# Both pooled halves ahead of the loop over heads, an encoder trunk on one core

## The chip, the cores and the metric

The kernel runs on one core of a Trainium2 chip. A core has five engines with an instruction queue each: TensorE (PE in the profile) multiplies matrices, VectorE (DVE), ScalarE (ACT) and GpSimd (POOL) work on tiles of 128 partitions, and SyncE (SP) issues most of the transfers. The metric is the time of one execution on the device, in microseconds (us).

## The reference, cut to what matters

A trunk of two layers over 512 tokens of 1024 channels, in float32. Each layer is a half-step feed-forward block, a mixing block and another half-step feed-forward block. The mixing block is what the change touches:

```python
proj = rmsnorm(x, mix_norm) @ w_in          # [v_pool 256 | q 768 | k 768 | v 768]
y_pool = multiscale_pool(v_pool, pool_w, pool_scale)
q, k = apply_partial_rope(q), apply_partial_rope(k)
y_attn = dilated_mixture_attention(q, k, v) # 12 heads of 64 channels
x = x + concat(y_pool, y_attn) @ w_out

def multiscale_pool(v):                      # windows 2, 4, 8, 16 for four groups of 64 channels
    mean_g = (running sum of v_g over the window) / (valid positions)
    return ((mean - v) @ pool_w_g) * pool_scale
```

## The kernel before, in words

The activations are held transposed: channels on the 128 partitions, the 512 tokens along the free axis. A tile of 128 channels is 128x512, and the 1024 mixed channels are eight tiles y[0] to y[7]: y[0] and y[1] are the two pooled halves, y[2] to y[7] the six pairs of heads. Each float32 product is made from operands that are split in a high and a low part, as three matmuls (`mm3`, lines 414 to 419: high x high, high x low, low x high). A split is two instructions: ScalarE copies the high part (line 435, or 387 for weights: `whi`), and VectorE subtracts it from the whole (line 438, or 390 for weights: `wlo`). Such second instructions are recorded as "rests" and are issued at the next `flush()`.

All engines run their queues in the order in which the program is written; no scheduler moves anything. In `mix(l)` that order is: `values` and `qk` of pair 0, then `pool(0)` and `qk(1, 0)`, each by `run`, which issues a generator's products in one piece; then the loop over 13 steps s of four quarters q. A step makes the scores and the exp of head s (`scores`; VectorE's pass with the row maxima is line 914, ScalarE's exp line 916), the transposes of the probabilities of head s-1 with their split (`weigh`: `ph` and `pl`), and the products with the values (`gather`). Between them `advance()` issues one piece (six matmuls) of the product that the table `fill` gives to the step: q or k of a later pair. In the last steps it also issues output products.

Three parts of the loop matter here:

- `pool(c)`: 24 matmuls (`pp_pool`), then VectorE's `v_pool` (line 983), then a chain on GpSimd: three memsets, running sums (line 992, two of them for c = 0 and four for c = 1), two scalings (lines 1004 and 1005) and a subtraction (line 1006) that gives `m_pool`. The generator stops at `yield "tail"`, and some yields later it splits the small weight (`pwh`, `pwl`) and `m_pool` (`dh_pool` on ScalarE, `dl_pool` on VectorE), and makes three matmuls (`po_pool`), from which ScalarE takes y[c].
- `qk(pr, s)`: 24 matmuls (`pp_q`, `pp_k`), VectorE's product with the cosines (`ra`, line 875) and shuffle (`rb`, 876), GpSimd's two instructions (lines 877 and 878), and the split `hl_q` or `hl_k`, which is then copied to the stacked operands by DMAs of SyncE.
- `prepare(c)` splits y[c] into `yh[c]` at the place that the table `plan` names, and `out(d, ks)` makes the products of output tile d with the mixed tiles ks, three matmuls for each, at the places of the table `work`. Both tables are keyed by (step, quarter).

The weights' order in the list of loads (`plain(*entry)`) is the order in which the products take them.

Of the kernel before, what the change touches and what calls it, by code (L numbers as in the profile page):

```python
# [78 lines left out]
def trunk(ctx: ExitStack, tc: tile.TileContext, a: dict):  # L79
    nc = tc.nc  # L80
# [168 lines left out]
    def plain(key, src, n):  # L249
        ld = Load(src, n)  # L250
        loads.append(ld)
        jobs.append(Job(key, n, [ld], lambda: ld.tile, done=free))
# [71 lines left out]
    def ffn_jobs(i, l):  # L324
        for n, u in enumerate(UNITS):
            if n == 0:
                for g in range(4):
                    plain(("c", i, l, g), a[f"gc{i}"][l, g], D)
                continue
            pj = product_jobs(i, l, u)  # L330
            dj = down_jobs(i, l, UNITS[n - 1]) if n else []
            for z, job in enumerate(pj):
                jobs.append(job)
                if n and z in DOWN_AT[n == len(UNITS) - 1]:
                    jobs.append(dj.pop(0))
            jobs.extend(dj)
        jobs.extend(down_jobs(i, l, UNITS[-1]))

    for l in range(DEPTH):
        ffn_jobs(1, l)  # L340
        vu = [[(("v", l, hf, g), a["wv"][l, hf, g], 768) for g in range(4)] for hf in range(2)]
        qk = [(("qk", l, p_, s), a["wqk"][l, p_, s], D) for p_ in range(NPAIR) for s in range(2)]
        pu = [(("p", l, c), a["wp"][l, c], D) for c in range(2)]
        wo = [(("o", l, d), a["wo"][l, d], D) for d in range(KD)]
        for entry in vu[0] + qk[:2] + vu[1] + pu[:1] + qk[2:] + pu[1:] + wo:
            plain(*entry)
        ffn_jobs(2, l)

# [84 lines left out]
    def split_later(dst, src, then=None, engine=nc.vector):  # L433
        hi, lo = dst
        nc.scalar.activation(hi, src, AF.Copy)

        def rest():
            engine.tensor_tensor(lo, src, hi.bitcast(F32), op=ALU.subtract)
            if then is not None:
                then()  # L440
        later.append(rest)
# [384 lines left out]
    def mix(l, norm, nxt):  # L826
# [5 lines left out]
        y = [None] * KD  # L832
        yh = [None] * KD
# [32 lines left out]
        def qk(pr, s, before=None, tag="A"):  # L866
            name = f"{'qk'[s]}_{nm}_{pr}"
            ps = bank(tag, f"pp_{name}")
            yield from project(take("qk", l, pr, s), ps)
            if before is not None:  # L870
                before()
                yield "tail"
            t = t2([P, S], F32, f"ra_{name}")
            sh = t2([P, S], F32, f"rb_{name}")
            nc.vector.tensor_tensor(t, ps, rc, op=ALU.mult)
            nc.vector.stream_shuffle(sh, ps, SWAP)
            nc.gpsimd.tensor_tensor(sh, sh, rsn, op=ALU.mult)
            nc.gpsimd.tensor_tensor(t, t, sh, op=ALU.add)
            hl = t4([P, 2, S], F32R, f"hl_{name}")
            yield "tail"  # L880
            if (pr, s) != (NPAIR - 1, 1):
                yield

            def stacks():
                for j in range(2):
                    hd = 2 * pr + j
                    src = hl[j * HD:(j + 1) * HD].bitcast(F32)
                    if s == 0:
                        st = t4([P, 2, S], F32R, f"qq_{nm}_{hd}")
                        nc.sync.dma_start(st[0:HD].bitcast(F32), src)  # L890
                        nc.sync.dma_start(st[HD:P].bitcast(F32), src)
                        qq[hd] = st
                    else:
                        st = t2([P, S], F32R, f"kk_{nm}_{hd}")
                        nc.sync.dma_start(st[0:HD].bitcast(F32), src[:, 0, :])
                        nc.sync.dma_start(st[HD:P].bitcast(F32), src[:, 1, :])
                        kk[hd] = st

            split_later(planes(hl), t, stacks)
# [66 lines left out]
        def prepare(c):  # L966
            if c in (1, 6, 7):
                yh[c] = (t2([P, S], F32R, f"yhh_{nm}_{c}"), t2([P, S], F32R, f"yhl_{nm}_{c}"))
            elif c in (2, 3):
                yh[c] = (t2([P, S], F32R, f"yhh_{nm}_{c}"), t2([P, S], F32R, f"yhl_{nm}_{c}"))  # L970
            else:
                yh[c] = planes(t4([P, 2, S], F32R, f"yh_{nm}_{c}"))
            split_later(yh[c], y[c], engine=nc.gpsimd if c in (0, 2, 3) else nc.vector)

        def pool(c, tag="A"):
            name = f"pool_{nm}_{c}"
            ps = bank(tag, f"pp_{name}")
            yield from project(take("p", l, c), ps)
            W = S + 16
            v = t4([P, W], F32, f"v_{name}")  # L980
            nc.gpsimd.memset(v[:, 0:8], 0.0)
            nc.gpsimd.memset(v[:, S + 8:W], 0.0)
            nc.vector.tensor_tensor(v[:, 8:S + 8], ps, norm.row, op=ALU.mult)
            ic = t2([P, S], F32, f"ic_{name}")
            nc.sync.dma_start(ic, a["icnt"][:, c])
            raw = t2([P, P], F32, f"pwr_{name}")
            nc.gpsimd.memset(raw, 0.0)
            for g in range(2):
                nc.sync.dma_start(raw[g * 64:(g + 1) * 64, g * 64:(g + 1) * 64], a["pool_w"][l, 2 * c + g])
            s = t4([P, W], F32, f"s_{name}")  # L990
            r = t4([P, W], F32, f"r_{name}")
            add = lambda o, i, sh, lo, n: nc.gpsimd.tensor_tensor(
                o[:, lo:lo + n], i[:, lo - sh[0]:lo - sh[0] + n], i[:, lo + sh[1]:lo + sh[1] + n], op=ALU.add)
            add(s, v, (1, 0), 1, W - 1)
            if c == 0:
                add(r, s, (1, 1), 8, S)
                first, second = s, r
            else:
                add(r, s, (1, 1), 2, W - 3)
                add(s, r, (2, 2), 4, W - 7)  # L1000
                add(r, s, (4, 4), 8, S)
                first, second = s, r
            m = t2([P, S], F32, f"m_{name}")
            nc.gpsimd.tensor_tensor(m[0:64], first[0:64, 8:S + 8], ic[0:64], op=ALU.mult)
            nc.gpsimd.tensor_tensor(m[64:P], second[64:P, 8:S + 8], ic[64:P], op=ALU.mult)
            nc.gpsimd.tensor_tensor(m, m, v[:, 8:S + 8], op=ALU.subtract)
            yield "tail"
            yield
            yield
            pw = (t2([P, P], F32R, f"pwh_{name}"), t2([P, P], F32R, f"pwl_{name}"))  # L1010
            split_later(pw, raw)
            yield
            yield
            d = (t2([P, S], F32R, f"dh_{name}"), t2([P, S], F32R, f"dl_{name}"))
            split_later(d, m)
            yield
            yield
            po_ = bank("D", f"po_{name}")
            mm3(po_, pw, 0, d, True, True)
            yc = t2([P, S], F32, f"y_{name}")  # L1020
            nc.scalar.activation(yc, po_, AF.Copy, scale=pscale(l, c))
            y[c] = yc

        wo, pso = {}, {}

        def out(d, ks):
            if d not in wo:
                wo[d] = take("o", l, d)
                pso[d] = bank("AABBCCAA"[d], f"po_{nm}_{d}")
            for k in ks:  # L1030
                mm3(pso[d], wo[d], k * P, yh[k], k == 0, k == 7)
# [16 lines left out]
        def run(gen):  # L1048
            live.append(gen)
            while True:  # L1050
                flush()
                if advance()[-1] is not None:
                    break
# [9 lines left out]
        run(qk(0, 1, tag="C"))  # L1063
        run(values(1))
        run(pool(0, tag="C"))
        run(qk(1, 0, tag="C"))
        fill = [qk(1, 1)]
        for p_ in range(2, NPAIR):
            fill += [qk(p_, 0), qk(p_, 1)]
        fill += [pool(1)]  # L1070

        plan = {(7, 3): (2,), (8, 2): (3,), (9, 1): (0,), (10, 0): (4,), (10, 2): (5,), (12, 0): (1,), (12, 2): (6,)}
        work = {(10, 0): ((0, (0, 2)),), (10, 1): ((1, (0, 2)),), (10, 2): ((0, (3, 4)),), (10, 3): ((1, (3, 4)),),
# [3 lines left out]
        state["behind"] = True  # L1077
        for s in range(NH + 1):
            if s < len(fill):
# [21 lines left out]
        flush()  # L1101
        gather(NH - 1, 2)
        out(0, (6,))
        out(1, (1, 6))
        gather(NH - 1, 3)
        flush()
        normalise(NPAIR - 1)
        flush()
        prepare(7)
        flush()  # L1110
        out(2, (1, 6))
        out(3, (6,))
        out(4, (0, 2, 3, 4, 5, 1, 6))
        for d in range(KD):
# [78 lines left out]
```

## Time and profile before

| | us |
|---|---|
| median of three runs | 1872.42 (1870.88 to 1872.94) |
| the profiled execution, its own time | 1871.56 |
| its span in the trace | 1869.2 |
| TensorE busy | 1851.1 (99%) |
| VectorE busy | 1403.0 (75%) |
| ScalarE busy | 934.2 (50%) |
| GpSimd busy | 117.6 (6%) |

The span is what the trace covers of the execution; the rest lies around it. The mixing block is a stretch of each of the two layers, and its loop over heads lies from 424.5 to 555.1 in layer 0. The busy time of TensorE counts overlapping matmuls once, so the rate at which matmuls start is read from their start times.

### The profile page before, as it was taken

The page shows a single profiled execution, that of the slowest core. Times are in us where ns is not written, and L with a number is a line of the kernel's source. Part 1 is how long each engine was busy: PE and PEld are TensorE (multiplying, and loading weights), DVE is VectorE, ACT ScalarE, POOL GpSimd, SP SyncE. Part 2 cuts the span into 40 slices and gives each one's busy share as a digit, 9 for nine tenths or more (in the row PEclk, how much of TensorE's full clock was granted, in tenths as well). Part 3 has the DMA queues.
Part 4 walks back from the last instruction along what each step waited for, and adds up shares of the span by engine and source line. Part 5 has one row for each costly group of instructions (what it writes and reads, how often), then busy time and mean ns, then how long its engine had stood idle before and what let it go on. Part 6 is the DMA issues. An engine that isn't in the chain of part 4 may idle for free.

```text
span 1869.2 us, 23006 instructions
## 1 busy us (share of the span) xinstructions
PE 1851.1 (99%) x8735; PEld 1537.4 (82%) x8735; DVE 1403.0 (75%) x1983; ACT 934.2 (50%) x1440; POOL 117.6 (6%) x104
## 2 busy tenths in 40 slices
PE   9999999999999999999999999999999999999998
PEld 7788888898878888888888888888887788888888
DVE  5888777748887887677698677775688697777675
ACT  6444444526665554444464344344467565444344
POOL 0000000014230000000000000000323200000000
PEclk8999999999999999999999999999999999999999
DMA  4332333144442232333403332230544223323321
GB/s 188 124 102 79 112 124 111 43 126 122 113 142 96 74 105 99 113 106 108 136 23 118 119 102 97 95 130 17 147 123 126 102 85 119 114 89 102 102 79 46
DMA packets 59375, 194.33 MB, mean 104 GB/s; under 512 B 8001, under 2 KB 8129, under 8 KB 59265
## 3 DMA queue, kind: packets, MB, share of 16 engines
q1 hardware_dynamic: 58720, 192.05, 32.0%
q8 instruction: 69, 1.13, 0.3%
q10 hardware_dynamic: 432, 0.56, 0.1%
q14 instruction: 42, 0.34, 0.1%
q0 software_dynamic: 112, 0.26, 0.0%
HBM read 171.87 MB, written 2.10 MB: 93 GB/s over the span
## 4 chain that ended last, share of the span: by engine, by line
PE 92%; DVE 5%; issue 1%; ACT 1%; DMA 0%; DVEq 0%; POOLq 0%; POOL 0%; ACTq 0%
PE pd_f L419 9%; PE pd_f L417 8%; PE pd_f L418 8%; PE px_f L710 7%; PE px_f L707 7%; PE px_f L709 7%; PE pz_f L710 6%; PE pz_f L707 6%; PE pz_f L709 6%; PE pv_m L844 4%; PE ps_m L911 2%; PE pt_m L924 2%; PE pt_f L656 2%; PE pc_f L752 2%; PE pc_f L754 2%; PE pc_f L753 2%
## 5 line engine op out<-in xcount | busy, mean ns | idle before, releaser
L390 DVE TENSOR_TENSOR wlo<-raw,whi 128x1024 fp32r<-128x1024 f32 (+2 forms) x414 | 489.9, 1189 | 50.8 <-ACT whi L387 46.5
L387 ACT ACTIVATE whi<-raw 128x1024 fp32r<-128x1024 f32 (+2 forms) x414 | 413.6, 1023 | 225.0 <-DVE wlo L390 67.7
L419 PE MATMUL pd_f<-ah_f,wlo 128*128 128x512 f32 (+1 forms) x736 | 281.2, 382 | 1.8 <-DVE wlo L390 1.7
L417 PE MATMUL pd_f<-ah_f,whi 128*128 128x512 f32 (+1 forms) x736 | 280.8, 382 | 0.0
L418 PE MATMUL pd_f<-al_f,whi 128*128 128x512 f32 (+1 forms) x736 | 279.6, 380 | 0.0
L802 DVE SCALAR_TENSOR_TENSOR x<-pd_f,x 128x512 f32<-128x512 f32 x184 | 127.0, 690 | 168.5 <-PE pd_f L419 165.0
L648 ACT ACTIVATE c_f<-c_f,rcol_n 128x256 f32<-128x256 f32 x120 | 61.2, 510 | 232.5 <-DVE c_f L689 87.5
L419 PEld LDWEIGHTS pd_f<-ah_f,wlo 128*128 128x128 f32 x736 | 138.3, 188 | 31.9 <-DVE wlo L390 6.1
L418 PEld LDWEIGHTS pd_f<-al_f,whi 128*128 128x128 f32 x736 | 138.5, 188 | 26.2
L417 PEld LDWEIGHTS pd_f<-ah_f,whi 128*128 128x128 f32 x736 | 138.5, 188 | 25.5
L710 PE MATMUL px_f<-wlo,sh_n 128*128 128x512 f32 x320 | 124.6, 389 | 1.7 <-DVE wlo L390 1.7
L710 PE MATMUL px_f<-wlo,ah_n 128*128 128x512 f32 x320 | 124.6, 389 | 0.0
L709 PE MATMUL px_f<-whi,sl_n 128*128 128x512 f32 x320 | 124.5, 389 | 0.0
L707 PE MATMUL px_f<-whi,sh_n 128*128 128x512 f32 x320 | 124.5, 389 | 0.0
L707 PE MATMUL px_f<-whi,ah_n 128*128 128x512 f32 x320 | 124.5, 389 | 0.0
L709 PE MATMUL px_f<-whi,al_n 128*128 128x512 f32 x320 | 124.5, 389 | 0.0
L707 PE MATMUL pz_f<-whi,sh_n 128*128 128x512 f32 x320 | 124.5, 389 | 0.0
L709 PE MATMUL pz_f<-whi,sl_n 128*128 128x512 f32 x320 | 124.5, 389 | 0.0
L710 PE MATMUL pz_f<-wlo,sh_n 128*128 128x512 f32 x320 | 124.5, 389 | 0.0
L916 ACT ACTIVATE e_m<-e_m,nmx_m 128x512 f32<-128x512 f32 x96 | 69.4, 723 | 81.3 <-DVE nmx_m L914 81.0
L914 DVE CUSTOM_DVE_ANT_0 e_m<-ps_m,gbias 128x512 f32<-128x512 f32 x96 | 65.9, 686 | 30.7 <-PE ps_m L911 29.9
L554 POOL TENSOR_TENSOR rcol_n<-rcol_n,npow 128x4 f32<-128x4 f32 x6 | 7.4, 1228 | 1197.0 <-DVE rcol_n L553 1197.0
(222 smaller groups left out, 3683.1 us busy)
## 6 DMA issues: line engine op xcount, KB each, us to landing
raw<-in_gu SPq DMA_DIRECT2D x160, 512.0 KB, 3.3
raw<-in_dn SPq DMA_DIRECT2D x80, 512.0 KB, 3.3
raw<-in_wqk SPq DMA_DIRECT2D x24, 512.0 KB, 5.4
qq_m<-hl_q_m SPq DMA_DIRECT2D x48, 256.0 KB, 4.3
raw<-in_wo SPq DMA_DIRECT2D x16, 512.0 KB, 5.0
raw<-in_gc SPq DMA_DIRECT2D x15, 512.0 KB, 4.2
raw<-in_wv SPq DMA_DIRECT2D x16, 384.0 KB, 3.1
kk_m<-hl_k_m SPq DMA_DIRECT2D x48, 128.0 KB, 2.3
```

The lines of the kernel that those rows point to most:

```text
L387: nc.scalar.activation(hi[:, o:e], raw[:, o:e], AF.Copy)
L390: nc.vector.tensor_tensor(lo[:, o:e], raw[:, o:e], hi[:, o:e].bitcast(F32), op=ALU.subtract)
L417: nc.tensor.matmul(ps, hi[:, o:o + P], act[0], start=start, stop=False)
L418: nc.tensor.matmul(ps, hi[:, o:o + P], act[1], start=False, stop=False)
L419: nc.tensor.matmul(ps, lo[:, o:o + P], act[0], start=False, stop=stop)
L707: nc.tensor.matmul(ps, bh, hi[:, o], start=(k == 0 and p in (1, 2, 5)), stop=False, skip_group_check=True)
L709: nc.tensor.matmul(ps, bl, hi[:, o], start=False, stop=False, skip_group_check=True)
L710: nc.tensor.matmul(ps, bh, lo[:, o], start=False, stop=(k == 3), skip_group_check=True)
L802: nc.vector.scalar_tensor_tensor(x[d], ps, 0.5, x[d], op0=ALU.mult, op1=ALU.add)
L844: nc.tensor.matmul(ps[t][:, :384], h[k][p_][:, t * P:(t + 1) * P], q_[:, o:o + 384], start=(k == 0 and n == 0), stop=(k == KD - 1 and n == 2))
L914: nc.vector.tensor_tensor_reduce(e, ps, gbias[:, o:o + S], -0.125, 3.0e38, ALU.add, ALU.min, nmx[hd][:, it:it + 1])
L916: nc.scalar.activation(e, e, AF.Exp, bias=nmx[hd][:, it:it + 1], scale=-1.0, accum_out=den[hd][:, it:it + 1])
```

## The change

`pool(1)` is run right after `pool(0)`, ahead of the loop, and leaves the table `fill`; its weight moves up in the list of loads. The tail of `pool` waits four yields instead of two before it goes on. The rests of all splits of mixed tiles 0 to 5 go to GpSimd, before only those of tiles 0, 2 and 3. The tables `plan` and `work` are written anew: output tiles 0 and 1 take their products three matmuls a quarter in steps 9, 10 and 11 (before: 24 in step 10, 6 in step 11, some in step 12), and the product with y[1] moves up. The number of matmuls is the same.

```diff
--- before
+++ after
@@ -342,7 +342,7 @@
         qk = [(("qk", l, p_, s), a["wqk"][l, p_, s], D) for p_ in range(NPAIR) for s in range(2)]
         pu = [(("p", l, c), a["wp"][l, c], D) for c in range(2)]
         wo = [(("o", l, d), a["wo"][l, d], D) for d in range(KD)]
-        for entry in vu[0] + qk[:2] + vu[1] + pu[:1] + qk[2:] + pu[1:] + wo:
+        for entry in vu[0] + qk[:2] + vu[1] + pu + qk[2:] + wo:
             plain(*entry)
         ffn_jobs(2, l)
 
@@ -970,7 +970,7 @@
                 yh[c] = (t2([P, S], F32R, f"yhh_{nm}_{c}"), t2([P, S], F32R, f"yhl_{nm}_{c}"))
             else:
                 yh[c] = planes(t4([P, 2, S], F32R, f"yh_{nm}_{c}"))
-            split_later(yh[c], y[c], engine=nc.gpsimd if c in (0, 2, 3) else nc.vector)
+            split_later(yh[c], y[c], engine=nc.gpsimd if c < 6 else nc.vector)
 
         def pool(c, tag="A"):
             name = f"pool_{nm}_{c}"
@@ -1005,8 +1005,8 @@
             nc.gpsimd.tensor_tensor(m[64:P], second[64:P, 8:S + 8], ic[64:P], op=ALU.mult)
             nc.gpsimd.tensor_tensor(m, m, v[:, 8:S + 8], op=ALU.subtract)
             yield "tail"
-            yield
-            yield
+            for _ in range(4):
+                yield
             pw = (t2([P, P], F32R, f"pwh_{name}"), t2([P, P], F32R, f"pwl_{name}"))
             split_later(pw, raw)
             yield
@@ -1063,17 +1063,18 @@
         run(qk(0, 1, tag="C"))
         run(values(1))
         run(pool(0, tag="C"))
+        run(pool(1, tag="C"))
         run(qk(1, 0, tag="C"))
         fill = [qk(1, 1)]
         for p_ in range(2, NPAIR):
             fill += [qk(p_, 0), qk(p_, 1)]
-        fill += [pool(1)]
-
-        plan = {(7, 3): (2,), (8, 2): (3,), (9, 1): (0,), (10, 0): (4,), (10, 2): (5,), (12, 0): (1,), (12, 2): (6,)}
-        work = {(10, 0): ((0, (0, 2)),), (10, 1): ((1, (0, 2)),), (10, 2): ((0, (3, 4)),), (10, 3): ((1, (3, 4)),),
-                (11, 1): ((0, (5,)),), (11, 3): ((1, (5,)),),
-                (12, 0): ((2, (0, 2, 3)),), (12, 1): ((2, (4, 5)), (0, (1,))),
-                (12, 2): ((3, (0, 2, 3)),), (12, 3): ((3, (4, 5, 1)),)}
+
+        plan = {(7, 2): (2,), (8, 0): (0,), (8, 3): (3,), (9, 1): (1,), (10, 0): (4,), (10, 3): (5,), (12, 2): (6,)}
+        work = {(9, 0): ((0, (0,)),), (9, 1): ((0, (2,)),), (9, 2): ((1, (0,)),), (9, 3): ((1, (2,)),),
+                (10, 0): ((0, (3,)),), (10, 1): ((0, (1,)),), (10, 2): ((1, (3,)),), (10, 3): ((1, (1,)),),
+                (11, 0): ((0, (4,)),), (11, 1): ((1, (4,)),), (11, 2): ((0, (5,)),), (11, 3): ((1, (5,)),),
+                (12, 0): ((2, (0, 2, 3)),), (12, 1): ((2, (1, 4, 5)),),
+                (12, 2): ((3, (0, 2, 3)),), (12, 3): ((3, (1, 4, 5)),)}
         state["behind"] = True
         for s in range(NH + 1):
             if s < len(fill):
@@ -1101,14 +1102,14 @@
         flush()
         gather(NH - 1, 2)
         out(0, (6,))
-        out(1, (1, 6))
+        out(1, (6,))
         gather(NH - 1, 3)
         flush()
         normalise(NPAIR - 1)
         flush()
         prepare(7)
         flush()
-        out(2, (1, 6))
+        out(2, (6,))
         out(3, (6,))
         out(4, (0, 2, 3, 4, 5, 1, 6))
         for d in range(KD):
```

On GpSimd, at the head of the loop of layer 0, the rows from pool(0)'s last instruction on stand so before (`m_pool_m_0` is pool(0)'s result, `rb_q_m_1` and `ra_q_m_1` belong to q of pair 1, `rb_k_m_1` and `ra_k_m_1` to its k):

```order
L1006 TENSOR_TENSOR m_pool_m_0_3356<-m_pool_m_0_3356,v_pool_m_0_3342 128x512
L877 TENSOR_TENSOR rb_q_m_1_3396<-rb_q_m_1_3396,rsn_m_2936 128x512
L878 TENSOR_TENSOR ra_q_m_1_3395<-ra_q_m_1_3395,rb_q_m_1_3396 128x512
L877 TENSOR_TENSOR rb_k_m_1_3478<-rb_k_m_1_3478,rsn_m_2936 128x512
L878 TENSOR_TENSOR ra_k_m_1_3477<-ra_k_m_1_3477,rb_k_m_1_3478 128x512
```

and so after the change:

```order
L1006 TENSOR_TENSOR m_pool_m_0_3356<-m_pool_m_0_3356,v_pool_m_0_3342 128x512
L981 MEMSET v_pool_m_1_3391 128x8
L982 MEMSET v_pool_m_1_3391 128x8
L987 MEMSET pwr_pool_m_1_3397 128x128
L992 TENSOR_TENSOR s_pool_m_1_3401<-v_pool_m_1_3391 128x527
L992 TENSOR_TENSOR r_pool_m_1_3402<-s_pool_m_1_3401 128x525
L992 TENSOR_TENSOR s_pool_m_1_3401<-r_pool_m_1_3402 128x521
L992 TENSOR_TENSOR r_pool_m_1_3402<-s_pool_m_1_3401 128x512
L1004 TENSOR_TENSOR m_pool_m_1_3407<-s_pool_m_1_3401,ic_pool_m_1_3395 64x512
L1005 TENSOR_TENSOR m_pool_m_1_3407<-r_pool_m_1_3402,ic_pool_m_1_3395 64x512
L1006 TENSOR_TENSOR m_pool_m_1_3407<-m_pool_m_1_3407,v_pool_m_1_3391 128x512
L877 TENSOR_TENSOR rb_q_m_1_3451<-rb_q_m_1_3451,rsn_m_2936 128x512
```

The ten instructions of pool(1) stand between pool(0)'s last one and the rows of q of pair 1, where nothing stood; the row of `ra_q_m_1` follows.

On VectorE at the same place, around the score pass with the index 0_2 (head 0, third quarter; line 914), before:

```order
L438 TENSOR_TENSOR dl_pool_m_0_3411<-m_pool_m_0_3356,dh_pool_m_0_3410 128x512
L390 TENSOR_TENSOR wlo_3415<-raw_3306,whi_3414 128x1024
L914 ISA e_m_0_2_3443,nmx_m_0_3403<-ps_m_0_2_3440,gbias 128x512
L914 ISA nmx_m_0_3403 128x1
L438 TENSOR_TENSOR hl_q_m_1_3401<-ra_q_m_1_3395,hl_q_m_1_3401 128x512
L914 ISA e_m_0_3_3468,nmx_m_0_3403<-ps_m_0_3_3465,gbias 128x512
L914 ISA nmx_m_0_3403 128x1
L875 TENSOR_TENSOR ra_k_m_1_3477<-pp_k_m_1_3413,rc_m_2935 128x512
```

and after:

```order
L914 ISA e_m_0_2_3504,nmx_m_0_3458<-ps_m_0_2_3501,gbias 128x512
L914 ISA nmx_m_0_3458 128x1
L438 TENSOR_TENSOR hl_q_m_1_3456<-ra_q_m_1_3450,hl_q_m_1_3456 128x512
L914 ISA e_m_0_3_3526,nmx_m_0_3458<-ps_m_0_3_3523,gbias 128x512
L914 ISA nmx_m_0_3458 128x1
L438 TENSOR_TENSOR dl_pool_m_1_3515<-m_pool_m_1_3407,dh_pool_m_1_3514 128x512
L875 TENSOR_TENSOR ra_k_m_1_3536<-pp_k_m_1_3474,rc_m_2935 128x512
```

`dl_pool` of pool(0) and a `wlo` have moved ahead of this stretch, and `dl_pool` of pool(1) has come in behind the rest of `hl_q_m_1` and a score pass.

On TensorE, at the beginning of step 1 (scores of head 1), after:

```order
L911 MATMUL ps_m_1_0_3545<-kk_m_1_3235,qq_m_1_3151 128x512 x2
L417 MATMUL po_pool_m_1_3551<-dh_pool_m_1_3514,pwh_pool_m_1_3471 128x512
L418 MATMUL po_pool_m_1_3551<-dl_pool_m_1_3515,pwh_pool_m_1_3471 128x512
L419 MATMUL po_pool_m_1_3551<-dh_pool_m_1_3514,pwl_pool_m_1_3472 128x512
L417 MATMUL pp_q_m_2_3557<-h_n_0_2779,whi_3415 128x512
```

The three matmuls of `po_pool_m_1` are new there; before, the projection `pp_q_m_2` follows the scores directly.

On VectorE, in steps 9 and 10, before (`pl_m_8_2` is the split of the transposed probabilities of head 8, third quarter):

```order
L438 TENSOR_TENSOR pl_m_8_2_4582<-pt_m_8_2_4576,ph_m_8_2_4581 128x512
L983 TENSOR_TENSOR v_pool_m_1_4600<-pp_pool_m_1_4506,rstd_n_3110 128x512
L933 RECIPROCAL rd_m_8_4629<-den_m_8_4359 128x4
L934 COPY rden_m_4_4628<-rd_m_8_4629 128x4x64
L914 ISA e_m_10_0_4639,nmx_m_10_4635<-ps_m_10_0_4636,gbias 128x512
L914 ISA nmx_m_10_4635 128x1
L438 TENSOR_TENSOR pl_m_8_3_4626<-pt_m_8_3_4620,ph_m_8_3_4625 128x512
L914 ISA e_m_10_1_4675,nmx_m_10_4635<-ps_m_10_1_4672,gbias 128x512
L914 ISA nmx_m_10_4635 128x1
L964 TENSOR_TENSOR y_m_3_4407<-y_m_3_4407,rdt_m_3_4645 128x512
L438 TENSOR_TENSOR yh_m_4_4650<-y_m_2_4149,yh_m_4_4650 128x512
L438 TENSOR_TENSOR pl_m_9_0_4670<-pt_m_9_0_4664,ph_m_9_0_4669 128x512
```

and after:

```order
L438 TENSOR_TENSOR pl_m_8_2_4648<-pt_m_8_2_4642,ph_m_8_2_4647 128x512
L390 TENSOR_TENSOR wlo_4634<-raw_4447,whi_4633 128x1024
L933 RECIPROCAL rd_m_8_4673<-den_m_8_4425 128x4
L934 COPY rden_m_4_4672<-rd_m_8_4673 128x4x64
L914 ISA e_m_10_0_4683,nmx_m_10_4679<-ps_m_10_0_4680,gbias 128x512
L914 ISA nmx_m_10_4679 128x1
L438 TENSOR_TENSOR pl_m_8_3_4670<-pt_m_8_3_4664,ph_m_8_3_4669 128x512
L914 ISA e_m_10_1_4710,nmx_m_10_4679<-ps_m_10_1_4707,gbias 128x512
L914 ISA nmx_m_10_4679 128x1
L964 TENSOR_TENSOR y_m_3_4475<-y_m_3_4475,rdt_m_3_4689 128x512
L438 TENSOR_TENSOR pl_m_9_0_4705<-pt_m_9_0_4699,ph_m_9_0_4704 128x512
```

`v_pool_m_1` and the `yh` split have left VectorE's list, and a `wlo` stands where `v_pool_m_1` stood.

## Rows read from the trace of the kernel before

**Rows 1.** The page: busy us, share of the span and instructions.

```profile
PE 1851.1 (99%) x8735; PEld 1537.4 (82%) x8735; DVE 1403.0 (75%) x1983; ACT 934.2 (50%) x1440; POOL 117.6 (6%) x104
```

**Rows 2.** Windows, loop: us, PE, PEld, DVE, ACT, POOL busy, PEclk, DMA share, GB/s.

```profile
424.50:521.30 96.80, 96.78 (x493) 77.95 (x492) 81.75 (x176) 66.14 (x133) 29.34 (x22) 1.00 0.44 113
521.30:555.10 33.80, 31.55 (x160) 24.17 (x159) 29.44 (x58) 23.75 (x50) 13.75 (x13) 1.00 0.57 185
```

**Rows 3.** Waits of PE, 521.3 to 555.1: us in total, times, longest.

```profile
PE po_m L944 <- DVE pl_m L438: 1.5, 2, 1.3
PE po_m L940 <- DVE y_m L957: 0.4, 1, 0.4
PE pt_m L924 <- DVE pl_m L438: 0.3, 1, 0.3
```

**Rows 4.** Timeline of PE at its longest wait: start, us, instruction, idle time before.

```profile
545.00 0.40 PE L940 MATMUL po_m<-ph_m,v_m 128*128 128x512 f32 x1
546.67 0.44 PE L944 MATMUL po_m<-pl_m,v_m 128*64 128x512 f32 x1 [1.27 <-DVE pl_m L438]
```

**Rows 5.** Timeline of DVE in step 10.

```profile
537.66 1.75 DVE L438 TENSOR_TENSOR yh_m<-y_m,yh_m 128x512 fp32r<-128x512 f32 x1
...
539.94 1.72 DVE L390 TENSOR_TENSOR wlo<-raw,whi 128x1024 fp32r<-128x1024 f32 x1
...
543.39 1.21 DVE L390 TENSOR_TENSOR wlo<-raw,whi 128x1024 fp32r<-128x1024 f32 x1
```

**Rows 6.** Timeline of POOL, pool(1) in steps 10 and 11.

```profile
532.78 1.19 POOL L992 TENSOR_TENSOR s_pool_m<-v_pool_m 128x527 f32<-128x527 f32 x1 [2.41 <-DVE rd_m L933]
...
538.94 1.64 POOL L1005 TENSOR_TENSOR m_pool_m<-r_pool_m,ic_pool_m 64x512 f32<-64x512 f32 x1
540.65 2.16 POOL L1006 TENSOR_TENSOR m_pool_m<-m_pool_m,v_pool_m 128x512 f32<-128x512 f32 x1
```

**Rows 7.** Timeline of PE: first of qk(1,0)'s 24 matmuls, and the loop's first.

```profile
419.11 0.39 PE L417 MATMUL pp_q_m<-h_n,whi 128*128 128x512 f32 x1
...
424.55 0.62 PE L911 MATMUL ps_m<-kk_m,qq_m 128*128 128x512 f32 x2
```

**Rows 8.** Timeline of POOL at the head of the loop.

```profile
424.50 1.30 POOL L1005 TENSOR_TENSOR m_pool_m<-r_pool_m,ic_pool_m 64x512 f32<-64x512 f32 x1
425.88 1.29 POOL L1006 TENSOR_TENSOR m_pool_m<-m_pool_m,v_pool_m 128x512 f32<-128x512 f32 x1
427.13 1.30 POOL L877 TENSOR_TENSOR rb_q_m<-rb_q_m,rsn_m 128x512 f32<-128x512 f32 x1
428.51 1.62 POOL L878 TENSOR_TENSOR ra_q_m<-ra_q_m,rb_q_m 128x512 f32<-128x512 f32 x1
```

**Rows 9.** Timeline of ACT at the head of the loop.

```profile
430.16 0.63 ACT L435 ACTIVATE hl_q_m<-ra_q_m 128x512 fp32r<-128x512 f32 x1 [0.46 <-POOL ra_q_m L878]
```

**Rows 10.** Timeline of DVE at the head of the loop.

```profile
431.74 0.68 DVE L438 TENSOR_TENSOR hl_q_m<-ra_q_m,hl_q_m 128x512 fp32r<-128x512 f32 x1
```

**Rows 11.** Timeline of PE: first scores of step 9 and of step 10.

```profile
521.30 0.62 PE L911 MATMUL ps_m<-kk_m,qq_m 128*128 128x512 f32 x2
...
532.60 0.62 PE L911 MATMUL ps_m<-kk_m,qq_m 128*128 128x512 f32 x2
```

**Rows 12.** Timeline of DVE in step 9: pl of (8,0) and (8,1).

```profile
526.97 0.69 DVE L438 TENSOR_TENSOR pl_m<-pt_m,ph_m 128x512 fp32r<-128x512 f32 x1 [0.73 <-ACT ph_m L435]
...
530.14 0.69 DVE L438 TENSOR_TENSOR pl_m<-pt_m,ph_m 128x512 fp32r<-128x512 f32 x1
```

**Rows 13.** Timeline of PE near the kernel's start.

```profile
23.84 10.39 PE L550 MATMUL ms_n<-ones,sq_n 128*128 128x1 f32 x64
...
34.10 0.77 PE L752 MATMUL pc_f<-whi,ah_n 128*128 128x512 f32 x1
...
37.66 0.40 PE L754 MATMUL pc_f<-wlo,ah_n 128*128 128x512 f32 x1
```

**Rows 14.** Windows near the kernel's start, columns as in rows 2.

```profile
34.00:36.00 2.00, 2.00 (x7) 1.61 (x7) 1.69 (x6) 0.01 (x1) 1.48 (x2) 0.50 0.00 0
...
50.00:54.00 4.00, 2.56 (x12) 1.80 (x11) 4.00 (x5) 1.61 (x3) 0.00 (x0) 1.00 0.33 89
```

## The prediction

> All times are us of layer 0; layer 1 repeats the pattern 895.9 later, so a gain or loss per layer counts twice.
>
> **What bounds the kernel now.** I read the page's busy times first. TensorE is busy for 1851.1 of the span, 99% [rows 1]; VectorE has a quarter of the span free, GpSimd nearly all. So only TensorE's few gaps can be won, and any instruction that makes TensorE wait is lost in full. Next the windows of the loop over heads: in steps 0 to 8 TensorE works 96.78 of 96.80, in steps 9 to 12 it works 31.55 of 33.80 [rows 2]. The 2.25 of idle time there is the whole prize in this loop. The waits view of those steps names four stalls, nearly all for VectorE's split of a transposed probability tile, pl_m [rows 3]. A stall costs a little more than its idle time: the two matmuls in [rows 4] start 1.67 apart where a 128x512 matmul takes 0.227 (see [rows 7] below), so 1.44 are lost for 1.27 of idle time, 0.17 more. With four stalls, 2.25 + 0.7 = 2.9 per layer.
>
> Why is VectorE late there? Its timeline shows a split yh_m of 1.75 and a weight split wlo of 1.72; the next wlo, of the same shape, takes 1.21 [rows 5]. The long ones fall in the time in which GpSimd makes pool(1), 532.78 to 542.81, and GpSimd's own instructions are stretched in turn: 1.64 and 2.16 [rows 6], against 1.30 and 1.29 for the same two of pool(0) [rows 8]. So a GpSimd tensor_tensor and a VectorE tensor_tensor that reads two SBUF tiles delay one another. The pl_m split, which reads PSUM and SBUF, keeps 0.68 in the same stretch.
>
> **What the change does in steps 9 to 12.** pool(1) leaves: 24 matmuls of step 9, GpSimd's chain of ten, VectorE's v_pool and the d split. 12 of out's matmuls come into step 9 instead. The yh rests of tiles 1, 4 and 5 go to GpSimd, which has room now, and leave VectorE (three of 0.68, one of them 1.75 as stretched). Steps 10 to 12 then lose VectorE work, and I expect no wait there. Step 9 is different: TensorE has 12 matmuls less, 12 x 0.227 = 2.72, but VectorE's list up to pl of (8,1) is the same. Step 9 lasts 11.30 now [rows 11]. Without the 0.3 that it waits now and 2.72 less, TensorE would be through at 521.30 + 8.3 = 529.6. But the pl split of (8,1) begins at 530.14 and ends at 530.83 [rows 12], its matmul is next to last in the step, and so the step ends at 530.83 + 0.23 + 0.17 = 531.2, 1.6 late. A wlo now stands where v_pool stood, 0.53 longer (1.21 - 0.68), part of which reaches step 10: I take 1.9 for the new wait. The relief is 2.9 - 1.9 = 1.0 per layer. Bounds: 2.9 if no wait remains (VectorE pauses 0.73 for ScalarE before the pl of (8,0) [rows 12], so its list can move forward in part), and 0.1 if the whole wlo of 1.21 is added to the 1.6.
>
> **What it does at the head of the loop.** This is the larger term. GpSimd works its queue in order. Before, m of pool(0) ends at 425.88 + 1.29 = 427.17, and rb and ra of q of pair 1 follow at once, done at 430.13 [rows 8]; ScalarE waits 0.46 for them [rows 9] and TensorE not at all. After the change, pool(1)'s ten instructions stand between. Three are memsets, of 128 columns at most: 0.3, an estimate from 1.29 for 512. The seven others ran in the trace: the first five from 532.78 to 538.94, 6.16 [rows 6], and the last two unstretched 1.29 each [rows 8], 8.7 in all. Then rb, 1.38 from start to start, and ra, 1.29 when unstretched. Sum: 427.17 + 0.3 + 8.7 + 2.7 = 438.9 for ra, if VectorE never stands in the way. But in that time VectorE has two wlo and the d split of pool(0) to do, all with two SBUF inputs. By the trace a wlo beside GpSimd stretched GpSimd's instruction from 1.29 to 2.16, 0.87 more [rows 6], and a split of 512 columns stretches one by 0.33 (1.62 against 1.29, the ra of [rows 8]). 2 x 0.87 + 0.33 = 2.1, so ra ends at 441.0. If each VectorE instruction put its whole length on top, 2 x 1.21 + 0.68 = 3.1, it would be 442.0.
>
> Behind ra stand, in order: hl_q on ScalarE, 0.63 [rows 9]; and in VectorE's queue the rest of hl_q (0.68), the score pass of (0,3) (0.68) and dl of pool(1) (0.68, as the hl_q split of [rows 10]). dl of pool(1) is the operand of the second matmul of po_pool. 0.63 + 3 x 0.68 = 2.67, so dl is there at 443.7. TensorE comes to it at step 1, quarter 0. Its loop starts 24 matmuls later than before, since pool(1)'s product now stands ahead: from the 24 matmuls of [rows 7], 424.55 + 5.44 = 429.99. Ahead of it are 38 matmuls (five quarters' scores of two, 24 of qk(1,1), three of pool(0)'s po_pool and the first of its own), 8.63, so TensorE is there at 438.6. It waits 5.1 there; by the unblocked sum 3.0, by whole lengths 6.1. I take 5.0. The probabilities of (0,3), which the first transposes need next, are done by then too, as ScalarE's exp follows the score pass while dl runs. So there is one stall per layer, not two. The four yields instead of two in pool's tail move TensorE's request later, but not by enough: the 38 matmuls include them.
>
> The Trainium skill has a rule on this, SBUF — State Buffer, section "Who interferes with whom": a VectorE instruction with two SBUF inputs contends with a GpSimd instruction that reads SBUF, and the loser fully blocks. The trace agrees that they delay one another; by the rule in its strict form each of the three instructions would add its whole length, the 6.1 case, which would make the time 2.2 longer than my sum. The rows show 0.87 for a 1.21, since the GpSimd instruction may have had part of its work behind it, so I stay with those.
>
> **The clock.** A stall of 5 may let TensorE's clock fall. Rows show this at the start of the kernel only: after 10.39 of one-column matmuls [rows 13] the granted clock was 0.50, the lower of the two levels, 1.2 GHz [rows 14], and the eight matmuls from 34.10 to 37.66 took 3.56 where full speed takes 1.82, a loss of 1.7. In 50 to 54, in which TensorE was busy for 2.56 of 4.00, the clock stayed at 1.00 [rows 14]. A 5 us stall lies between those two. I count one fall in the two layers, +1.7, with none and two as bounds.
>
> **Sum.** (5.0 - 1.0) x 2 = 8.0. The profiled execution took 1871.56, 0.86 below the median of 1872.42; 1871.56 + 8.0 + 0.86 = 1880.4, and with one fall of the clock 1882.1. Without a fall 1880.4, with two 1883.8.
>
> **Rivals.**
> 1. *Short stall, full relief; no change to be measured.* VectorE's wlo fall between GpSimd's instructions and block nothing (stall 3.0), and step 9's list moves forward (relief 1.0 to 2.9). Per layer +2.0 to +0.1: 1872.6 to 1876.4. For it: wlo instructions wait for ScalarE's whi and may come late. Against: they stand in VectorE's queue ahead of the score pass that TensorE needs.
> 2. *The head is hidden; faster.* Nothing waits if ra ends by 438.6 - 2.67 = 435.9, that is 3.0 earlier than by the unblocked sum: GpSimd's chain would have to run in 5.7 instead of 8.7. The trace has these seven only once in a layer, beside a busy VectorE, so their lengths may be inflated: but even at the 1.19 of the first of them [rows 6] seven take 8.3. Then the relief alone is left: 2.0 to 5.8, 1866.6 to 1870.4.
> 3. *The waits only change places in steps 9 to 12.* GpSimd's yh rests block VectorE's splits as pool(1) did, relief 0.1, while the head stalls at 6.1: +12, with the clock up to 1887.8.
>
> **Chances.** Head stall of about 5 (with rival 3 as its worse end): 0.75, of which 0.2 with no fall of the clock, 0.35 with one, 0.2 with two or with the worse end. Rival 1: 0.13. Rival 2: 0.12. A measurement of this kernel can tell about 0.2%, 3.7, from no change. So slower 0.75, same 0.13, faster 0.12. The range leaves out rival 2 and the lower half of rival 1: 1874 to 1887.
>
> **What would show it.** In the profile after: GpSimd without a pause from 420 to 441; ScalarE's hl_q waiting several us for GpSimd's ra, once in each layer; TensorE's matmul of po_pool at line 418 waiting for dl of pool(1), about 5, twice, with the exps of head 0 late behind hl_q on ScalarE. In steps 9 to 12 splits at 0.68 and wlo at 1.21 again, and 1 to 2 of idle time, mostly before the matmul of pl(8,1). After each head stall the granted clock may read below 1.00 for a few us. I am wrong if TensorE passes po_pool without a wait, if GpSimd's seven take under 6, or if steps 9 to 12 give back more than 2.9, which would need a gain that no row here shows.

## The result and the profile after

The changed kernel took 1882.74 us (median of six runs, 1880.35 to 1883.24) against 1871.87 for the kernel before (six runs, 1870.56 to 1872.94): 1.006 times as long, with an interval of 1.005 to 1.007. It is slower, by 10.9. The profiled execution has a span of 1881.2, 12.0 more than before.

The page's busy line and its chain, after, beside [rows 1]:

```profile
PE 1854.9 (99%) x8735; PEld 1541.3 (82%) x8735; DVE 1397.4 (74%) x1977; ACT 935.2 (50%) x1440; POOL 126.6 (7%) x110
...
PE 89%; DVE 3%; issue 3%; POOL 2%; ACT 1%; DMA 1%; DVEq 0%; POOLq 0%; ACTq 0%
```

The chain of the kernel before:

```profile
PE 92%; DVE 5%; issue 1%; ACT 1%; DMA 0%; DVEq 0%; POOLq 0%; POOL 0%; ACTq 0%
```

TensorE executes as many matmuls as before, but its busy time is 3.8 longer, which speaks for a slower clock. GpSimd, which had no share in the chain before, now holds 2% of it. The waits of TensorE over the whole span name the place (us in total, times, longest):

```profile
PE po_pool_m L417 <- ACT dh_pool_m L435: 8.3, 2, 4.1
PE pt_m L924 <- DVE pl_m L438: 3.2, 4, 0.9
```

The first line is new: twice, once in each layer, 4.1 at the head of the loop. TensorE's timeline there, in layer 0:

```profile
437.81 0.61 PE L911 MATMUL ps_m<-kk_m,qq_m 128*128 128x512 f32 x2
442.56 0.80 PE L417 MATMUL po_pool_m<-dh_pool_m,pwh_pool_m 128*128 128x512 f32 x1 [4.14 <-ACT dh_pool_m L435]
443.29 0.80 PE L418 MATMUL po_pool_m<-dl_pool_m,pwh_pool_m 128*128 128x512 f32 x1
443.88 0.63 PE L419 MATMUL po_pool_m<-dh_pool_m,pwl_pool_m 128*128 128x512 f32 x1
...
448.56 0.40 PE L417 MATMUL pp_q_m<-h_n,whi 128*128 128x512 f32 x1
```

TensorE waits for the high part of pool(1), and behind the wait its matmuls take 0.63 and more until 448.56, where they are at 0.40 again. The waiting operand is ScalarE's; ScalarE's timeline shows why it was late:

```profile
440.65 0.63 ACT L435 ACTIVATE hl_q_m<-ra_q_m 128x512 fp32r<-128x512 f32 x1 [5.37 <-POOL ra_q_m L878]
441.19 0.71 ACT L916 ACTIVATE e_m<-e_m,nmx_m 128x512 f32<-128x512 f32 x1
441.80 0.19 ACT L916 ACTIVATION_READ_ACCUMULATOR e_m<-e_m,nmx_m 128x1 f32 x1
441.90 0.61 ACT L435 ACTIVATE dh_pool_m<-m_pool_m 128x512 fp32r<-128x512 f32 x1
```

`dh_pool` did not have to wait for its own operand: pool(1)'s last instruction on GpSimd had ended at 438.06 (below). It stands in ScalarE's queue behind `hl_q`, which waits 5.37 for GpSimd's `ra` (0.46 in [rows 9]). And GpSimd comes to `ra` only behind pool(1):

```profile
425.76 1.29 POOL L1006 TENSOR_TENSOR m_pool_m<-m_pool_m,v_pool_m 128x512 f32<-128x512 f32 x1
...
427.23 2.01 POOL L992 TENSOR_TENSOR s_pool_m<-v_pool_m 128x527 f32<-128x527 f32 x1
429.31 1.39 POOL L992 TENSOR_TENSOR r_pool_m<-s_pool_m 128x525 f32<-128x525 f32 x1
...
434.53 1.29 POOL L1005 TENSOR_TENSOR m_pool_m<-r_pool_m,ic_pool_m 64x512 f32<-64x512 f32 x1
435.89 2.17 POOL L1006 TENSOR_TENSOR m_pool_m<-m_pool_m,v_pool_m 128x512 f32<-128x512 f32 x1
...
439.36 1.26 POOL L878 TENSOR_TENSOR ra_q_m<-ra_q_m,rb_q_m 128x512 f32<-128x512 f32 x1
```

In [rows 8] the `ra` of the same pair began at 428.51; here it begins at 439.36. VectorE's timeline shows both kinds of delay, two `wlo` and the split of pool(0) beside GpSimd and the rest of `hl_q` that waits for ScalarE's part:

```profile
427.09 1.23 DVE L390 TENSOR_TENSOR wlo<-raw,whi 128x1024 fp32r<-128x1024 f32 x1 [1.25 <-POOL m_pool_m L1006]
428.23 1.56 DVE L438 TENSOR_TENSOR dl_pool_m<-m_pool_m,dh_pool_m 128x512 fp32r<-128x512 f32 x1
...
434.62 2.28 DVE L390 TENSOR_TENSOR wlo<-raw,whi 128x1024 fp32r<-128x1024 f32 x1
...
441.32 0.69 DVE L438 TENSOR_TENSOR hl_q_m<-ra_q_m,hl_q_m 128x512 fp32r<-128x512 f32 x1 [3.81 <-ACT hl_q_m L435]
```

The `wlo` from 434.62 to 436.90 lies across two instructions of GpSimd: it ends 1.07 later than its 1.21 [rows 5] would have it, and the second of them, at 435.89, 0.88 later than its 1.29. Windows of the stall, of what follows it and of step 9, after (columns as in [rows 2]):

```profile
438.20:443.00 4.80, 0.66 (x2) 0.29 (x1) 1.68 (x4) 2.20 (x5) 2.34 (x2) 0.86 0.00 0
443.50:447.00 3.50, 3.50 (x9) 2.62 (x10) 1.57 (x5) 1.90 (x4) 2.35 (x2) 0.50 1.00 225
...
534.35:544.57 10.22, 8.61 (x46) 6.47 (x44) 8.54 (x18) 8.25 (x16) 5.57 (x4) 1.00 0.85 218
```

The granted clock falls within the stall and is 0.50, the 1.2 GHz level, behind it. Step 9 (the last line) is 10.22 long where it was 11.30 [rows 11], with 12 matmuls less. TensorE waits twice in it, and VectorE once, for `hl_k`:

```profile
540.46 0.63 PE L924 MATMUL pt_m<-ident,e_m 128*128 128x128 f32 x4 [0.68 <-DVE pl_m L438]
543.64 0.63 PE L924 MATMUL pt_m<-ident,e_m 128*128 128x128 f32 x4 [0.93 <-DVE pl_m L438]
...
538.61 1.10 DVE L438 TENSOR_TENSOR hl_k_m<-ra_k_m,hl_k_m 128x512 fp32r<-128x512 f32 x1 [0.84 <-ACT hl_k_m L435]
```

### The profile page after: what moved, and what is told of

The parts are those of the page before. It is cut to its first block, busy times and chain, and to the rows that moved or that the text cites. A ratio compares the mean times of both kernels' runs of the same rounds, so it can differ in the third digit from the quotient of the medians.

```text
span 1881.2 us, 23019 instructions
## 1 busy us (share of the span) xinstructions
PE 1854.9 (99%) x8735; PEld 1541.3 (82%) x8735; DVE 1397.4 (74%) x1977; ACT 935.2 (50%) x1440; POOL 126.6 (7%) x110
## 4 chain that ended last, share of the span: by engine, by line
PE 89%; DVE 3%; issue 3%; POOL 2%; ACT 1%; DMA 1%; DVEq 0%; POOLq 0%; ACTq 0%
PE pd_f L419 8%; PE pd_f L417 8%; PE pd_f L418 8%; PE px_f L710 7%; PE px_f L707 7%; PE px_f L709 7%; PE pz_f L710 6%; PE pz_f L707 6%; PE pz_f L709 6%; PE pv_m L844 3%; PE pt_f L656 2%; PE pt_m L924 2%; PE ps_m L911 2%; PE pc_f L752 2%; PE pc_f L754 1%
```

## The experiments

All times below were taken beside runs of the kernel before on the same chip (median 1870.91 in the first four runs, 1870.95 in the last three). The changed kernel itself was not run again with them, and the runs of the kernel before that stand beside it had 1871.87, so a difference from its 1882.74 is uncertain by about 1. The theory: pool(1)'s chain in GpSimd's queue makes `ra` late, the in-order queues of ScalarE and VectorE carry that to TensorE, and TensorE's clock falls behind the stall. The rivals: the product is asked for too early; the two engines' delaying of one another is what costs, wherever the chain stands; the clock would fall anyway.

**q of pair 1 ahead of pool(1).**

```diff
         run(pool(0, tag="C"))
-        run(pool(1, tag="C"))
         run(qk(1, 0, tag="C"))
+        run(pool(1, tag="C"))
```

(and the weight's place in the list of loads likewise)

> The changed kernel with one thing moved: q of pair 1 is run between the two pooled halves, so that GpSimd has rb and ra of q of pair 1 ahead of pool(1)'s ten instructions; everything else as changed. Theory (GpSimd's order makes ScalarE and VectorE wait, and through them TensorE): the head stall of about 4.8 per layer and the fall of the clock behind it (7.0 per layer together in the profile after) go; what may be left is a shorter wait for k of pair 1, whose two GpSimd instructions now stand behind pool(1), up to 1.2 per layer. With the relief of 1.0 per layer kept: 1869.8 without that wait, 1872.3 with it. Rival (it is the pooled product ahead of the loop, or GpSimd and VectorE delaying one another, whatever the order): 1878 or more.

Measured: 1876.66, 1.0026 of before (1.0015 to 1.0037). Neither number. The large stall is gone, but not all of it; TensorE's timeline at the first quarter of step 0:

```profile
433.44 0.50 PE L417 MATMUL po_pool_m<-dh_pool_m,pwh_pool_m 128*128 128x512 f32 x1 [1.32 <-ACT dh_pool_m L435]
434.25 0.50 PE L418 MATMUL po_pool_m<-dl_pool_m,pwh_pool_m 128*128 128x512 f32 x1 [0.31 <-DVE dl_pool_m L438]
```

This is the product of the other half, pool(0). Its `dh_pool` stands behind the same `hl_q` on ScalarE:

```profile
432.24 0.63 ACT L435 ACTIVATE hl_q_m<-ra_q_m 128x512 fp32r<-128x512 f32 x1 [9.24 <-POOL ra_q_m L878]
432.77 0.61 ACT L435 ACTIVATE dh_pool_m<-m_pool_m 128x512 fp32r<-128x512 f32 x1
```

In the kernel before, ScalarE has the two in the other order, this one and then the `hl_q` of [rows 9]:

```profile
427.44 0.62 ACT L435 ACTIVATE dh_pool_m<-m_pool_m 128x512 fp32r<-128x512 f32 x1
```

So the same mechanism holds with the halves exchanged, and the wait that I allowed for, at k of pair 1, was the wrong one. The clock falls here too, behind pauses of 1.32 and 0.31:

```profile
432.00:435.50 3.50, 1.87 (x7) 1.24 (x7) 2.50 (x5) 2.49 (x4) 0.98 (x5) 1.00 0.23 50
435.50:439.00 3.50, 3.50 (x10) 2.70 (x9) 1.09 (x3) 2.63 (x5) 3.27 (x4) 0.51 0.99 227
```

This execution, at 1878.46, is the slowest of the seven, with a mean granted clock of 0.993 where the other six have 0.995 or 0.996. So the clock may have cost less in those; no trace shows it.

**The product later.**

```diff
-            for _ in range(4):
+            for _ in range(4 if c == 0 else 10):
                 yield
```

> The changed kernel with pool(1)'s tail waiting ten yields instead of four, so that the three matmuls of po_pool of pool(1) come in step 2 instead of step 1. Theory (hl_q, which waits for GpSimd's ra, holds up ScalarE's exps behind it): TensorE still stalls in step 1, now at the first transposes of head 0, for the exp of (0,3); it gets there about 1.1 later than to po_pool, so some 3.8 of stall and the fall of the clock stay: 1880 to 1882. Rival (the wait is for po_pool's operand alone, which is asked for too early): the stall is gone, 1870 to 1873.

Measured: 1881.89 (1879.91 to 1883.26), 1.0055 of before (1.0042 to 1.0067). The stall has moved to the transposes of head 0, which wait for ScalarE's exp behind `hl_q`:

```profile
443.15 0.33 PE L924 MATMUL pt_m<-ident,e_m 128*128 128x128 f32 x1 [2.17 <-ACT e_m L916]
444.63 0.33 PE L924 MATMUL pt_m<-ident,e_m 128*128 128x128 f32 x1 [1.15 <-ACT e_m L916]
```

2.17 + 1.15 = 3.3 of idle time, 3.8 from start to start. The rival of a product that is asked for too early falls: whatever TensorE asks for next was behind the same instruction.

**Work for the stall.**

```diff
             po_ = bank("D", f"po_{name}")
+            if c == 1:
+                for _ in range(20):
+                    nc.tensor.matmul(po_, pw[0], h[0][0], start=True, stop=True)
             mm3(po_, pw, 0, d, True, True)
```

> The changed kernel with 20 matmuls of 128x512 (4.54) added on TensorE ahead of po_pool of pool(1), into the bank that po_pool then overwrites; they have no use but to keep TensorE working while it would wait, and leave the result as it is. Theory (the stall itself is 4.8 per layer, and the clock's fall behind it costs another 2.2 to 2.5 per layer): the filler lies in the stall, the clock stays at 1.00, and the time falls by 4.4 to 5.0 to 1877.7 to 1878.3. Rival (the clock falls whatever TensorE does there, or its fall costs nothing on the path): 1882 to 1883, or more by what of the filler doesn't fit.

Measured: 1878.09 (1876.77 to 1879.28), 1.0037 of before (1.0023 to 1.005): with 40 matmuls more the kernel is 4.65 below the changed one, or 3.7 when each is set against the kernel before beside it. The windows show the clock at 1.00 throughout:

```profile
437.00:443.00 6.00, 5.83 (x26) 4.51 (x26) 2.15 (x6) 2.67 (x6) 3.08 (x3) 1.00 0.06 14
443.00:447.00 4.00, 4.00 (x20) 3.28 (x21) 2.32 (x7) 2.36 (x6) 2.58 (x2) 1.00 0.99 225
```

So the fall of the clock comes from the stall. In the traces the first two steps of layer 0 are 2.3 shorter than the changed kernel's (the table below).

**Rests of tiles 1, 4 and 5 on VectorE.**

```diff
-            split_later(yh[c], y[c], engine=nc.gpsimd if c < 6 else nc.vector)
+            split_later(yh[c], y[c], engine=nc.gpsimd if c in (0, 2, 3) else nc.vector)
```

> The changed kernel with the rests of mixed tiles 1, 4 and 5 back on VectorE; all else as changed. Theory (the relief of 1.0 per layer comes from pool(1)'s chain and from the tables; in step 9 VectorE's list decides, and the rest of tile 1 comes into it): 0.7 more in step 9 of each layer, 1884.1, and nothing in steps 10 and 11. Rival 1 (the rests on GpSimd carry the relief): 2 or more, 1884.7 to 1887. Rival 2 (GpSimd's rests delay VectorE's weight splits as much as they save): 1882.7 or less.

Measured: 1883.47 (1880.46 to 1884.56), 1.0062 of before (1.0049 to 1.0075); the median is 0.7 above the changed kernel's, or 1.7 when each is set against the kernel before beside it, and the runs of the two overlap, so the times do not decide between the expectations. The trace is clearer: step 9 is 10.81 long instead of 10.22, 0.6 more where 0.7 was expected, but step 10, in which nothing was expected, is 0.35 shorter; a wait of TensorE of 0.2 for a `pl` that the changed kernel has there is gone, and why is not shown. Over steps 9 to the end of the mixing block 0.41 per layer is lost.

**Both halves ahead of the values' second half.**

```diff
         run(qk(0, 1, tag="C"))
-        run(values(1))
         run(pool(0, tag="C"))
         run(pool(1, tag="C"))
+        run(values(1))
         run(qk(1, 0, tag="C"))
```

> The changed kernel with both pooled halves run ahead of the values' second half instead of behind it, so that GpSimd's two chains run beside the values' products (some 16 of TensorE, in which GpSimd has nothing to do now) and are through before q of pair 1 comes; all else as changed. Theory (the loss is only where the chain stands in GpSimd's queue): no wait at the head of the loop, no fall of the clock, the relief of 1.0 per layer is kept, and before's own 0.3 per layer at po_pool of pool(0) goes too: 2.0 to 2.6 below before, 1868.8 to 1869.4 where before is 1871.4. Rival (pooling ahead of the loop costs wherever it stands, as GpSimd's chain delays VectorE's splits of the values and the weights, and TensorE waits for those): a stall of 1 to 3 per layer in the values' products, 1871 to 1876.

Measured: 1869.44 (1867.14 to 1871.15), 0.999 of before (0.998 to 0.9999), 13.3 below the changed kernel, or 12.4 when each is set against the kernel before beside it. It is 1.5 below before, less than the 2.0 to 2.6 expected. GpSimd's chain is about as long there (10.6 from 413.79), and its instructions are stretched as much, but it is over at 424.4, before `rb` of q of pair 1 can begin:

```profile
413.79 1.56 POOL L992 TENSOR_TENSOR s_pool_m<-v_pool_m 128x527 f32<-128x527 f32 x1
...
420.65 2.34 POOL L1005 TENSOR_TENSOR m_pool_m<-r_pool_m,ic_pool_m 64x512 f32<-64x512 f32 x1
423.07 1.29 POOL L1006 TENSOR_TENSOR m_pool_m<-m_pool_m,v_pool_m 128x512 f32<-128x512 f32 x1
431.06 1.30 POOL L877 TENSOR_TENSOR rb_q_m<-rb_q_m,rsn_m 128x512 f32<-128x512 f32 x1 [6.69 <-DVE rb_q_m L876]
```

Between 395 and 600 TensorE waits three times, all in steps 9 to 12:

```profile
PE pt_m L924 <- DVE pl_m L438: 1.6, 2, 1.0
PE po_m L944 <- DVE pl_m L438: 0.2, 1, 0.2
```

So the engines' delaying of one another costs nothing here where nobody waits, and the rival that pooling ahead of the loop costs in any place falls.

**The same, with two weight splits on GpSimd.**

```diff
-            nc.vector.tensor_tensor(lo[:, o:e], raw[:, o:e], hi[:, o:e].bitcast(F32), op=ALU.subtract)
+            engine = nc.gpsimd if job.key[0] == "o" and job.key[2] in (2, 3) else nc.vector
+            engine.tensor_tensor(lo[:, o:e], raw[:, o:e], hi[:, o:e].bitcast(F32), op=ALU.subtract)
```

> As the run before (both halves ahead of the values' second half), and the wlo of output tiles 2 and 3, which VectorE makes in step 9 though the products need them in step 12 only, on GpSimd. Theory (the 1.9 that remain in step 9 are VectorE's list, with these two wlo of 1.21 in it): 1.0 to 1.9 less per layer, 2.0 to 3.8 below the run before, 1865.0 to 1867.4. Rival (GpSimd's two wlo, some 2.6 each, delay VectorE's rest of hl_k and GpSimd's own rests as much as they take away): no gain against the run before, 1868.8 to 1870.

Measured: 1867.24 (1865.59 to 1868.48), 0.9978 of before (0.9969 to 0.9988), 2.2 below the run before it. This is faster than both kernels. In the stretch from 528 to 600 two waits of TensorE are left, 0.9 in all, where the run before it has the three above, 1.8 in all:

```profile
PE pt_m L925 <- DVE pl_m L439: 0.7, 1, 0.7
PE po_m L945 <- DVE pl_m L439: 0.2, 1, 0.2
```

The wait that is gone is the second of step 9's two, which had a `wlo` ahead of it in VectorE's list. The first stays: its `pl` stands behind the rest of `hl_k`, for which VectorE pauses 0.84 here as in the changed kernel.

**The move of pool(1) alone**, with the tables and the rests of the kernel before (the four yields and the weight's place as changed; the diff shows the move):

```diff
+        run(pool(1, tag="C"))
         run(qk(1, 0, tag="C"))
...
-        fill += [pool(1)]
```

> One part of the change alone: pool(1) ahead of the loop with its four yields, but the tables and the rests of the kernel before. Theory (VectorE's list sets the length of step 9, so TensorE waits for what it has too little of): the head stall and the clock's fall as in the changed kernel, and step 9 waits 4.7 instead of 1.9, since the 12 matmuls that the new tables put there (2.7) are missing: 1888, more if the clock falls there too. Rival (the tables bring nothing; the relief comes from taking pool(1)'s chain away): 1882 to 1884.

Measured: 1886.3 (1885.0 to 1886.94), 1.0078 of before (1.0066 to 1.0091). Between the two numbers, nearer to the theory's: TensorE waits in step 9 for 3.4 from start to start rather than 4.7. But the theory's reason holds only in part. VectorE makes no `wlo` in step 9 there (the changed kernel has one at 540.24), and before the longest wait it has nothing to do for 1.39: it waits for `hl_k`, which ScalarE starts when GpSimd's `ra` of that k ends, so GpSimd's queue decides there and not the length of VectorE's list (TensorE, VectorE, ScalarE):

```profile
539.08 0.63 PE L924 MATMUL pt_m<-ident,e_m 128*128 128x128 f32 x4 [1.80 <-DVE pl_m L438]
...
537.64 0.69 DVE L438 TENSOR_TENSOR hl_k_m<-ra_k_m,hl_k_m 128x512 fp32r<-128x512 f32 x1 [1.39 <-ACT hl_k_m L435]
...
536.98 0.63 ACT L435 ACTIVATE hl_k_m<-ra_k_m 128x512 fp32r<-128x512 f32 x1 [1.08 <-POOL ra_k_m L878]
```

The stretches of layer 0 side by side, from the start times of the first scores of steps 0, 2 and 9 and of the first feed-forward matmul in TensorE's timeline:

| kernel | steps 0 and 1 | step 9 to the feed-forward block |
|---|---|---|
| before | 18.31 | 75.73 |
| changed | 26.03 | 68.58 |
| work for the stall | 23.71 | 68.59 |
| rests on VectorE | 25.23 | 68.99 |
| ahead of the values | 18.18 | 68.56 |
| and weights on GpSimd | 18.18 | 67.70 |
| move alone | 25.75 | 70.76 |

The rows don't all hold the same matmuls in a stretch: before and the two runs ahead of the values have three of a po_pool in the first, the others six (0.68 more), and the work for the stall has its 20 besides; before has 27 of pool(1) in the second, the others none (6.13 less). In changed, rests on VectorE and move alone the first stretch has the same instructions. Their 26.03, 25.23 and 25.75 lie 2.3, 1.5 and 2.0 above the run with the clock at 1.00, so the price of a fall is not one number: from the first matmul behind the stall until they take 0.40 again it is 6.0 in changed (442.56 to 448.56) and 5.2 in rests on VectorE (440.54 to 445.69).

Two things were not tested: the new tables with pool(1) left in the loop, and the chain left where the change puts it with `hl_q` moved back in ScalarE's queue.

## Why the prediction was right

The forecast was 1882.1, slower; 1882.74 was measured. By its own steps:

- **What bounds the kernel, and where the prize is.** Right. All that changed in the loop is TensorE's waits at the head of the loop and in steps 9 to 12, and the clock. Steps 2 to 8 last 78.43 before and 78.45 after.
- **GpSimd's chain.** Forecast 427.17 + 0.3 + 8.7 + 2.7, plus 2.1 for VectorE's instructions: `ra` done at 441.0. Measured 439.36 + 1.26 = 440.62. The seven instructions took from 427.23 to 438.02 (the start of `rb`), 10.8, against 8.7 without blocking: 2.1 of stretch, as taken, and in the forecast's parts: the first sum takes 2.01 where it took 1.19 [rows 6], the second 1.39 where it took 1.06 before, the subtraction 2.17 instead of 1.29, that is 0.82, 0.33 and 0.88 beside a `wlo`, the d split and a `wlo`. The strict reading of the Trainium skill's rule (SBUF — State Buffer, "Who interferes with whom") would have given 3.1. The rule that one of the two is blocked agrees with the trace all the same: VectorE's `wlo` beside them took 2.28 instead of 1.21, so it waited as well. The three ended one after the other: GpSimd's line 1005 at 435.82, the `wlo` at 436.90, GpSimd's line 1006 at 438.06.
- **The stall.** Forecast 5.0 per layer. The changed kernel's 26.03, less 18.86 (the 18.18 of the run without a stall, and 0.68), is 7.17; 2.32 of it is the clock (26.03 - 23.71). That leaves 4.85. The forecast named the second matmul of po_pool and VectorE's `dl_pool`; it was the first and ScalarE's `dh_pool`, which stands behind the same `hl_q`. `dl_pool` came 0.7 later, and the second matmul began at 443.29, 0.4 ahead of the forecast's 443.7, as `ra` was.
- **The relief in steps 9 to 12.** Forecast 1.0 per layer. Measured 75.73 - 6.13 - 68.58 = 1.02. The new wait in step 9 was forecast at 1.9; the step has 1.9, from 0.83 and 1.10 lost at two transposes, which wait until a pl split has read the bank that they write, not at the pl product that I named. That the number agrees is in part luck: the forecast had VectorE's list as the reason, but before the first of the two VectorE pauses 0.84 for `hl_k`, behind GpSimd's `ra`; only before the second does it work without a pause. The rests on GpSimd give 0.4 of the 1.0 (68.99 against 68.58); the move alone loses 1.2 there (70.76 against 69.60), so without the tables and the rests there is no relief, and by these runs the tables bring the larger part (70.76 to 68.99).
- **The clock.** This is the mis-sized term. Forecast: one fall in the two layers, 1.7. Measured: a fall in each, 2.3 in layer 0 and 2.2 in layer 1, so 4.5. The rows at the kernel's start gave a price that was near, if low; that I counted one instead of two was a choice between bounds, and it was the wrong one.
- **The sum.** 2 x (4.85 - 1.02 + 2.32) = 12.3, less 0.3 for the wait at pool(0)'s product that before has (18.31 against 18.18), is 12.0, the difference of the spans. The medians differ by 10.9; the forecast of 9.7 lies 1.2 below that and 2.3 below the spans, nearly all of it the clock. That 1882.1 comes within 0.7 of 1882.74 is luck in part: the kernel before came out at 1871.87 and not at the 1872.42 that the forecast started from, and the medians lie closer together than the spans. Layer 1 lies 915.9 later (first scores at 424.55 and 1340.45 before), not 895.9 as the prediction has it; no term rests on that. In layer 1 the two stretches give 7.0 of loss and 0.8 of relief.
- **The rivals.** The hidden head would have needed GpSimd's seven in 5.7: they took 10.8. The short stall would have needed VectorE's `wlo` to come between GpSimd's instructions: the one at 434.62 fell across two of them. The third rival has the spans' 12.0 as its sum without the clock, but not its terms: it wanted a stall of 6.1 and a relief of 0.1, and they were 4.85 and 1.02.

What stays open is why pauses of 1.32 and 0.31 let the clock fall in one run while 0.68 and 0.93 in step 9 did not, and why the low clock cost less in some runs than in others.

## What to carry to other kernels

Before an engine with little to do is given a long chain of work, read who stands behind it in that engine's queue, and follow the first of those through every queue that runs in order: the price here was not the chain, but the 2.6 us of rotary work behind it, and the splits and exps behind that. The same ten instructions cost 7 us per layer in one place and nothing 13 us earlier. When a stall on TensorE can't be avoided, its price includes the matmuls that follow it at the lower clock; here 20 matmuls a layer without a use were cheaper than the pause.

## What the runs showed of the hardware

- The clock fell to 0.50 after a pause of 4.14, and in another run after 1.32 and 0.31 in 3.50 with TensorE busy for 1.87 of it, while 2.56 of 4.00 [rows 14] and step 9's 8.61 of 10.22 left it at 1.00. The shorter stall cost an estimated 1.7 by the clock alone (half of the 3.5 at 0.51), as much as its 1.6 of idle time, in the one execution that was traced.
- A VectorE copy with one input was held up by GpSimd too. In the fastest version a copy of `rden` takes 0.29 at 528.36, ahead of GpSimd's next instruction (528.40), and 1.22 where it begins within GpSimd's second `wlo`; it ends at 539.06, 0.16 after that `wlo` (timelines of VectorE and GpSimd):

```profile
528.36 0.29 DVE L935 COPY rden_m<-rd_m 128x256 f32<-128x256 f32 x1
...
537.84 1.22 DVE L935 COPY rden_m<-rd_m 128x256 f32<-128x256 f32 x1
...
536.52 2.38 POOL L391 TENSOR_TENSOR wlo<-raw,whi 128x1024 fp32r<-128x1024 f32 x1
```
